# Down projection of a two-layer decoder trunk by seven half-size products instead of eight

## The chip, the cores and the metric

The kernel runs on one core of a Trainium2 chip. The metric is the device time of one launch in microseconds (us). Before the change it is 1261.44 us, the median of three runs from 1261.15 to 1261.61. A core has a matrix engine (TensorE; PE in the profile, its weight loads PEld), a vector engine (VectorE, DVE), a scalar engine (ScalarE, ACT), GpSimd (POOL), and SyncE (SP), which issues nearly all transfers here. TensorE writes its sums to PSUM, of which this kernel uses eight banks of 128 x 512 f32; everything else is in SBUF, and transfers (DMA) bring data from DRAM and back.

## The reference

Two layers (DEPTH = 2) on 512 tokens of width 1024, all f32. Each layer is attention (twelve heads of two kinds), a projection, and a SwiGLU feed-forward part between two RMS norms. The change is in the last of these:

```python
h = rms_norm(x, ffn_pre_g[l])
y = (jax.nn.silu(h @ w_gate[l]) * (h @ w_up[l])) @ w_down[l]
x = x + rms_norm(y, ffn_post_g[l])
```

w_gate and w_up are 1024 x 2816, w_down is 2816 x 1024. The last product, of a 512 x 2816 hidden matrix with w_down, is the down projection.

## The kernel before

Every product is done in three matmuls on rounded numbers: each f32 operand is split into a high part (a cast, type f32r) and a low part (operand minus high part), and high x high, high x low and low x high are summed in PSUM. A matmul takes 128 x 128 of one operand as weights and streams 128 x 512 of the other.

The weights come from DRAM in chunks of 512 KB (128 partitions x 1024 elements) through `load_w` (L245): SP issues the load into one of two landing buffers (`wr`, NRAW = 2), ScalarE casts it to `wh` (L257), VectorE subtracts to get `wl` (L258). `wh` and `wl` have three buffers each. A landing buffer is free for the next load when the subtraction is done; a `wh`/`wl` pair when TensorE's last matmul with it is done.

Feed-forward part of layer l: `gate(f)` and `up(f)` (L1195, L1198) compute the f-th 128 hidden columns for all 512 tokens, transposed (hidden columns on partitions), 24 matmuls each; `swiglu` (L1201) puts silu(gate) x up into one of eight work tiles (`half_tile`, tag w2) and splits it into `hh`, `hl`, which stay in SBUF: 22 of each. Then the down projection (L1241 to L1297). Output half 0 (512 columns) of the four token tiles t goes to four PSUM banks d0, half 1 to four banks d1. For each chunk of two f, `down_mm` does 24 matmuls (4 token tiles x 2 f x 3), 22 x 4 x 2 x 3 = 528 in a layer. When d0 is done ScalarE squares and sums it (`first_half`) while d1 runs; the last two chunks of d1 are done token tile by token tile, and the post-norm of each tile (`post_norm`, L304) runs beside the next tile's matmuls. In layer 0 the pre-norm and the transposes for layer 1's attention (`pre_norm`, `pre_T`) and its first product (`va`, with weights `wva`) follow in the same stretch.

In the attention part the order of instructions is fixed by a planner. In the feed-forward part, from the third f to the end of the down projection's loop, a scheduler of the compiler orders each engine's instructions (`pinned[0] = False`, L1229); each engine then runs its own list from top to bottom and waits on semaphores for the others.

## Time and profile before

| | |
|---|---|
| median of 3 runs | 1261.44 us |
| profiled execution | 1262.44 us, span 1260.6 us |
| TensorE busy | 1227.2 us, 97% of the span |
| VectorE, ScalarE, GpSimd busy | 52%, 42%, 17% |
| down projection, layer 0 | from 513.5 to some 632.5 us of the span |
| down projection, layer 1 | from 1131 to some 1255 us |
| loads of w_down | 44 chunks of 512 KB, 3.5 us from issue to landing (median) |
| transfers | 125.9 MB, 100 GB/s over the span |

A row of the trace gives start, duration, engine, line and what is written from what; `[3.73 <-PE d L204]` behind it says that the engine had been idle for 3.73 us and what ended that. TensorE's matmuls overlap in the pipeline, so a matmul that is shown with 389 ns takes less when others follow; the time from one start to the next is what counts.

### The profile page before, as it was taken

To read this page: it belongs to the slowest core of one execution; us is meant where nothing else is said; L and a number is where in the kernel's file an instruction comes from. 1 tells how busy PE (TensorE), PEld (TensorE's weight loads), DVE (VectorE), ACT (ScalarE), POOL (GpSimd) and SP (SyncE) were. 2 spreads that over 40 slices of the span, in tenths; PEclk is the share of its full clock that TensorE was granted. 3 is DMA by queue.
4 is the path that set the end of the run, shared out by engine and by line. 5 is a ranking of instruction groups with operands and counts; after the bars stand their busy time and mean duration, and the time that the engine had idled before them with its cause. 6 is when DMAs were issued, how large, how long until landed. Compare 5 with 4: busy or idle time off the path is not lost.

```text
span 1260.6 us, 15936 instructions
## 1 busy us (share of the span) xinstructions
PE 1227.2 (97%) x5949; PEld 1014.4 (80%) x5949; DVE 651.1 (52%) x1252; ACT 534.0 (42%) x1040; POOL 213.6 (17%) x254
## 2 busy tenths in 40 slices
PE   8999999999999999999999999999999999999998
PEld 5787877788888888888877878777988888888886
DVE  7697858673333333222458977685633333332224
ACT  5476667453222222212344757674522222222221
POOL 1302457320000000000243124672100000000001
PEclk9999999999999999999999999999999999999999
DMA  7333443403333334222513333433133333332222
GB/s 236 83 85 93 109 117 101 134 18 101 100 100 94 92 100 134 100 90 94 151 35 92 93 86 100 126 113 96 49 102 100 90 95 101 101 117 87 97 100 84
DMA packets 158717, 125.94 MB, mean 100 GB/s; under 512 B 7008, under 2 KB 134112, under 8 KB 158640
## 3 DMA queue, kind: packets, MB, share of 16 engines
q1 hardware_dynamic: 158496, 124.40, 33.0%
q8 instruction: 47, 0.77, 0.3%
q10 hardware_dynamic: 144, 0.52, 0.1%
q14 instruction: 30, 0.25, 0.1%
HBM read 114.32 MB, written 2.20 MB: 92 GB/s over the span
## 4 chain that ended last, share of the span: by engine, by line
PE 50%; issue 31%; DVE 13%; ACT 4%; POOL 1%; DMA 0%; DVEq 0%; POOLq 0%; SPq 0%; ACTq 0%
PE pj_g L204 10%; PE pj_u L204 10%; PE d L204 9%; PE o L204 4%; PE va L204 3%; PE pj_kf L204 2%; PE pj_kd L204 2%; PE pj_qf L204 1%; PE vb L204 1%; DVE t2kd L735 1%; PE ptf L209 1%; PE sf L204 1%; DVE ed L954 1%; PE of L204 1%; DVE ae L1033 1%
## 5 line engine op out<-in xcount | busy, mean ns | idle before, releaser
L204 PE MATMUL pj_g<-hT_h,wh_g 128*128 128x512 f32 (+1 forms) x384 | 142.9, 372 | 0.0
L204 PE MATMUL pj_g<-hT_h,wl_g 128*128 128x512 f32 (+1 forms) x384 | 142.6, 371 | 0.0
L204 PE MATMUL pj_g<-hT_l,wh_g 128*128 128x512 f32 (+1 forms) x384 | 142.6, 371 | 0.0
L204 PE MATMUL pj_u<-hT_h,wh_u 128*128 128x512 f32 (+1 forms) x368 | 140.1, 381 | 0.0
L204 PE MATMUL pj_u<-hT_l,wh_u 128*128 128x512 f32 (+1 forms) x368 | 139.8, 380 | 0.0
L204 PE MATMUL pj_u<-hT_h,wl_u 128*128 128x512 f32 (+1 forms) x368 | 139.7, 380 | 0.0
L258 DVE TENSOR_TENSOR wl_u<-wr_u,wh_u 128x1024 fp32r<-128x1024 f32 x44 | 53.9, 1225 | 149.8 <-ACT wh_u L257 149.8
L204 PE MATMUL d<-wh_d,hh 128*128 128x512 f32 x336 | 130.8, 389 | 0.0
L204 PE MATMUL d<-wh_d,hl 128*128 128x512 f32 x336 | 130.7, 389 | 0.0
L204 PE MATMUL d<-wl_d,hh 128*128 128x512 f32 x336 | 130.7, 389 | 0.0
L258 DVE TENSOR_TENSOR wl_d<-wr_d,wh_d 128x1024 fp32r<-128x1024 f32 x42 | 51.4, 1225 | 147.4 <-ACT wh_d L257 146.8
L257 ACT CAST wh_u<-wr_u 128x1024 fp32r<-128x1024 f32 x44 | 46.3, 1053 | 157.6 <-PE pj_g L204 147.8
L257 ACT CAST wh_d<-wr_d 128x1024 fp32r<-128x1024 f32 x42 | 44.2, 1054 | 157.6 <-PE d L204 134.3
L257 ACT CAST wh_g<-wr_g 128x1024 fp32r<-128x1024 f32 x44 | 46.3, 1053 | 146.2 <-issue 124.7
L1206 DVE TENSOR_TENSOR sg<-pj_u,sg 128x512 f32<-128x512 f32 x44 | 30.4, 692 | 141.4 <-PE pj_u L204 141.4
L204 PEld LDWEIGHTS pj_g<-hT_h,wl_g 128*128 128x128 f32 x384 | 72.4, 189 | 12.5
L204 PEld LDWEIGHTS pj_g<-hT_l,wh_g 128*128 128x128 f32 x384 | 72.3, 188 | 12.5
L204 PEld LDWEIGHTS pj_g<-hT_h,wh_g 128*128 128x128 f32 x384 | 72.3, 188 | 12.5
L204 PEld LDWEIGHTS pj_u<-hT_h,wh_u 128*128 128x128 f32 x368 | 69.3, 188 | 13.1
L204 PEld LDWEIGHTS pj_u<-hT_h,wl_u 128*128 128x128 f32 x368 | 69.1, 188 | 13.1
L204 PEld LDWEIGHTS pj_u<-hT_l,wh_u 128*128 128x128 f32 x368 | 69.2, 188 | 12.9
L204 PEld LDWEIGHTS d<-wh_d,hl 128*128 128x128 f32 x336 | 63.1, 188 | 13.2
(273 smaller groups left out, 2686.0 us busy)
## 6 DMA issues: line engine op xcount, KB each, us to landing
wr_g<-in_w_gate_dram SPq DMA_DIRECT2D x44, 512.0 KB, 3.8
wr_u<-in_w_up_dram SPq DMA_DIRECT2D x44, 512.0 KB, 3.8
wr_d<-in_w_down_dram SPq DMA_DIRECT2D x44, 512.0 KB, 3.5
wr_o<-in_w_out_dram SPq DMA_DIRECT2D x16, 512.0 KB, 4.3
wr_kd<-in_w_in_dram SPq DMA_DIRECT2D x8, 512.0 KB, 4.0
wr_qd<-in_w_in_dram SPq DMA_DIRECT2D x8, 512.0 KB, 4.2
...
wr_kf<-in_w_in_dram SPq DMA_DIRECT2D x8, 512.0 KB, 4.0
```

Source lines behind the costliest of these rows:

```text
L204: ins = PE.matmul(out, a, b, start=start, stop=stop)
L209: ins = PE.transpose(out, a, idn)
L257: A.copy(hi, raw)
L258: (eng or V).tensor_sub(lo, raw, hi.bitcast(F32))
L735: return V.tensor_mul(b["t2"], b["t2"], sinT)
L954: return V.scalar_tensor_tensor(e0, e0, b["r"][:, 0:1], e1, op0=ALU.mult, op1=ALU.add)
L1033: return V.tensor_scalar_mul(b["e"][:, :n], b["e"][:, :n], b["l"])
L1206: V.tensor_mul(sg, pu, sg)
```

## The change

The hidden matrix A (512 tokens x 2816) and w_down B (2816 x 1024) are each cut in four quarters, A11 (tokens 0 to 255, hidden columns 0 to 1407), A12, A21, A22 and B11, ..., and the output in four quarters of 256 tokens x 512 columns. One level of Strassen's scheme with 15 sums makes the four out of seven products of quarter size: with S1 = A21 + A22, S2 = S1 - A11, S3 = A11 - A21, S4 = A12 - S2 and T1 = B12 - B11, T2 = B22 - T1, T3 = B22 - B12, T4 = T2 - B21 (here with its sign turned), these are A11 B11, A12 B21, S2 T2, S1 T1, S3 T3, S4 B22 and A22 T4, and seven more sums put them together.

- *Gate/up:* f goes 0, 11, 1, 12, ... (`ORDER`), so that the four parts of a hidden block of 128 are there after each pair. `swiglu` then makes S1 to S4. A11, A12, S1 and S2 are split (`put`) into SBUF operands `op0`, `op1`, `op3`, `op2`; S3, S4 and A22 go to DRAM (`s_d`). `weight_sums` reads four 128 x 512 blocks of w_down, makes the four weight sums on VectorE and writes them to DRAM (`t_d`).
- *Down:* `product(banks, g, x)` multiplies operand `op{g}` (256 tokens) with weight side x (0 to 3 are `t_d`, 4 to 7 are quarters of w_down) over 11 blocks of 128 in six chunks, the last of half size; it fills two banks. A chunk of two blocks has 12 matmuls, a product 66. `reload` fetches S3, S4, A22 from DRAM and splits them into `op0`, `op1`, `op2` when these are free. Between products VectorE or ScalarE copies or sums the banks into `u`, `c11`, `u3`, `p5`. The norms of token tiles 0 and 1 come ahead of the seventh product, those of 2 and 3 at its end.

```diff
-TAIL = 4
+FH, TH = FT // 2, S // 2
+ORDER = [f + FT // 2 * z for f in range(FT // 2) for z in range(2)]
...
+TAIL = 3
...
-WSTAGS = ("hl12", "hl13", "hl14", "hl15")
...
+            t_d = dpool.tile([4, FH * P, S], F32, name=f"t_d{l}", tag="t_d")
+            s_d = dpool.tile([3, FH, P, TH], F32, name=f"s_d{l}", tag="s_d")
+            wd, opd = wd_d[l], {}
...
+            def put(g, f, src):
+                if f % 2 == 0:
+                    opd[g, f // 2] = operand(g, f // 2)
+                x = opd[g, f // 2][:, f % 2]
+                A.copy(x[:, 0], src)
+                V.tensor_sub(x[:, 1], src, x[:, 0].bitcast(F32))
+            def weight_sums(f):
+                b11, b12, b21, b22 = (half_tile(f"b{l}{f}{x}") for x in range(4))
+                for x, t in enumerate((b11, b12, b21, b22)):
+                    r = (f + FH * (x // 2)) * P
+                    nc.sync.dma_start(t, wd[r:r + P, CH[x % 2]])
+                V.tensor_sub(b11, b12, b11)
+                V.tensor_sub(b12, b22, b12)
+                V.tensor_sub(b22, b22, b11)
+                V.tensor_sub(b21, b21, b22)
+                for x, t in enumerate((b11, b22, b12, b21)):
+                    nc.sync.dma_start(t_d[x, f * P:(f + 1) * P], t)
...
+                if f < FH:
+                    first[f] = sg
+                    put(0, f, sg[:, :TH])
+                    return
+                f -= FH
+                a11, a21, a12, a22 = (x[:, c] for x in (first.pop(f), sg) for c in (slice(0, TH), slice(TH, S)))
+                put(1, f, a12)
+                nc.sync.dma_start(s_d[2, f], a22)
+                w = half_tile(f"s12{l}{f}")
+                s1, s2 = w[:, :TH], w[:, TH:]
+                V.tensor_add(s1, a21, a22)
+                V.tensor_sub(s2, s1, a11)
+                put(3, f, s1)
+                put(2, f, s2)
+                w = half_tile(f"s34{l}{f}")
+                s3, s4 = w[:, :TH], w[:, TH:]
+                V.tensor_sub(s3, a11, a21)
+                V.tensor_sub(s4, a12, s2)
+                nc.sync.dma_start(s_d[0:2, f].rearrange("x p n -> p x n"), w.rearrange("p (x n) -> p x n", x=2))
+                weight_sums(f)
...
-            for f in range(2, FT):
+            for f in ORDER[2:]:
...
-            def down_mm(bank, w, f, t):
-                tk = slice(t * P, (t + 1) * P)
-                for kk in range(2):
-                    mm(bank, hid[f + kk][0][:, tk], w[0][kk], f + kk == 0, False)
-                    mm(bank, hid[f + kk][0][:, tk], w[1][kk], False, False)
-                    mm(bank, hid[f + kk][1][:, tk], w[0][kk], False, f + kk == FT - 1)
...
-            d0 = [bank_t(f"d0{l}0"), bank_t(f"d0{l}1"), bank_s(f"d0{l}2"), bank_s(f"d0{l}3")]
-            d1 = [bank_g(f"d1{l}{t}") for t in range(NT)]
-            for f in range(0, FT, 2):
-                w = down_w(0, f)
-                for t in range(NT):
-                    down_mm(d0[t], w, f, t)
-            s2s = [first_half(t, d0[t], f"fp{l}") for t in range(NT)]
-            for f in range(0, FT - TAIL, 2):
-                w = down_w(1, f)
-                for t in range(NT):
-                    down_mm(d1[t], w, f, t)
...
+            def chunk_w(x, q, dst=None):
+                n = min(2, FH - 2 * q)
+                src = side(x)[2 * q * P:(2 * q + n) * P].rearrange("(k p) n -> p k n", p=P)
+                return load_w(src, [P, n, S], f"d{l}{x}{q}", dst=dst)
+            def product_mm(bank, g, q, w, m):
+                a = opd[g, q]
+                tk = slice(m * P, (m + 1) * P)
+                n = a.shape[1]
+                for k in range(n):
+                    s, e = q == k == 0, q == QN - 1 and k == n - 1
+                    mm(bank, a[:, k, 0, tk], w[0][:, k], s, False)
+                    mm(bank, a[:, k, 0, tk], w[1][:, k], False, False)
+                    mm(bank, a[:, k, 1, tk], w[0][:, k], False, e)
+            def product(banks, g, x, qs=None):
+                for q in qs or range(QN):
+                    w = chunk_w(x, q)
+                    for m in range(2):
+                        product_mm(banks[m], g, q, w, m)
+            def reload(g, s):
+                for q in range(QN):
+                    n = min(2, FH - 2 * q)
+                    raw = half_tile(f"rs{l}{s}{q}")[:, :n * TH].rearrange("p (k n) -> p k n", k=n)
+                    nc.sync.dma_start(raw, s_d[s, 2 * q:2 * q + n].rearrange("k p n -> p k n"))
+                    x = opd[g, q] = operand(g, q)
+                    A.copy(x[:, :, 0], raw)
+                    V.tensor_sub(x[:, :, 1], raw, x[:, :, 0].bitcast(F32))
+            QN = (FH + 1) // 2
+            A_, C_, B_ = ([mk(f"d{x}{l}{m}") for m in range(2)] for x, mk in (("a", bank_t), ("c", bank_s),
+                                                                             ("b", bank_g)))
+            name = f"fp{l}"
+            s2s, ys = {}, {}
+            product(A_, 0, 4)
+            u = [half_tile(f"u{l}{m}") for m in range(2)]
+            for m in range(2):
+                A.copy(u[m], A_[m])
+            product(C_, 1, 6)
+            reload(0, 0)
+            c11 = [half_tile(f"c11{l}{m}") for m in range(2)]
+            for m in range(2):
+                V.tensor_add(c11[m], C_[m], u[m])
+                s2s[m] = first_half(m, c11[m], name)
+            product(A_, 2, 1)
+            for m in range(2):
+                V.tensor_add(u[m], A_[m], u[m])
+            reload(1, 1)
+            product(B_, 3, 0)
+            p5, y, u3, y2 = (hp.tile([P, 2, S], F32, name=f"{x}{l}", tag=f"op3{q}") for q, x in enumerate(
+                ("p5", "y0", "u3", "y2")))
+            for m in range(2):
+                A.copy(p5[:, m], B_[m])
+            reload(2, 2)
+            for t in range(2):
+                ys[t] = y[:, t]
+                V.tensor_mul(ys[t], c11[t], g_fpost[:, CH[0]])
+            product(A_, 0, 2)
+            for m in range(2):
+                V.tensor_add(u3[:, m], A_[m], u[m])
+                V.tensor_add(u[m], p5[:, m], u[m])
+            product(B_, 1, 7)
+            last = l + 1 == DEPTH
+            for m in range(2):
+                V.tensor_add(u[m], B_[m], u[m])
+            for t in range(2):
+                post_norm(t, u[t], s2s[t], g_fpost, name, y=ys[t], store=last)
+                if not last:
+                    hs[t] = pre_norm(t, g_apre, f"a{l + 1}")
+            for m in range(2):
+                ys[2 + m] = y2[:, m]
+                V.tensor_add(ys[2 + m], u3[:, m], p5[:, m])
+                s2s[2 + m] = first_half(2 + m, ys[2 + m], name, z=1)
+                V.tensor_mul(ys[2 + m], ys[2 + m], g_fpost[:, CH[1]])
+            product(A_, 2, 3, range(QN - TAIL))
+            ws = [chunk_w(3, q) for q in range(QN - TAIL, QN)]
...
+            for m in range(2):
+                t = 2 + m
+                for w, q in zip(ws, range(QN - TAIL, QN)):
+                    product_mm(A_[m], 2, q, w, m)
+                    if m and not last and q == QN - TAIL:
+                        pre_T(0, hs[0], a)
+                c21 = half_tile(f"c21{l}{m}")
+                V.tensor_add(c21, A_[m], u3[:, m])
+                post_norm(t, c21, s2s[t], g_fpost, name, z=0, y=ys[t], store=last)
+                if not last:
+                    hs[t] = pre_norm(t, g_apre, a)
...
```

The compiled order shows where the sums stand. First VectorE, before, at the change from half 0 to half 1 of layer 0 (`wl_d0` and two more figures is layer 0's chunk: half, then f; the last figures are buffer numbers):

```order
L258 TENSOR_TENSOR wl_d0018_4949<-wr_d0018_4947,wh_d0018_4948 128x1024
L258 TENSOR_TENSOR wl_d0020_4979<-wr_d0020_4977,wh_d0020_4978 128x1024
L258 TENSOR_TENSOR wl_d010_5021<-wr_d010_5019,wh_d010_5020 128x1024
L258 TENSOR_TENSOR wl_d012_5051<-wr_d012_5049,wh_d012_5050 128x1024
L258 TENSOR_TENSOR wl_d014_5081<-wr_d014_5079,wh_d014_5080 128x1024
L258 TENSOR_TENSOR wl_d016_5111<-wr_d016_5109,wh_d016_5110 128x1024
```

Then VectorE now, from the third product to the fourth (`wl_d01` and a figure are chunks of the third product, `wl_d00` of the fourth; `op` and `rs` belong to a reload; `da` are the two banks of the third product):

```order
L259 TENSOR_TENSOR wl_d015_5305<-wr_d015_5303,wh_d015_5304 128x512
L1327 TENSOR_TENSOR op21070_5462<-rs021_5460,op21070_5462 128x2x256
L1327 TENSOR_TENSOR op22071_5467<-rs022_5465,op22071_5467 128x2x256
L1327 TENSOR_TENSOR op23072_5472<-rs023_5470,op23072_5472 128x2x256
L1327 TENSOR_TENSOR op24073_5477<-rs024_5475,op24073_5477 128x2x256
L1346 TENSOR_TENSOR u00_5067<-da00_4959,u00_5067 128x512
L1346 TENSOR_TENSOR u01_5068<-da01_4960,u01_5068 128x512
L259 TENSOR_TENSOR wl_d000_5349<-wr_d000_5347,wh_d000_5348 128x1024
L259 TENSOR_TENSOR wl_d001_5367<-wr_d001_5365,wh_d001_5366 128x1024
```

Before, subtractions follow each other with nothing between; now the two sums of the finished banks stand ahead of the next product's first subtraction, here as after products 2, 5 and 6.

ScalarE, before, at the same change of halves (`junk` are the squares of the four finished banks):

```order
L257 CAST wh_d0020_4978<-wr_d0020_4977 128x1024
L257 CAST wh_d010_5020<-wr_d010_5019 128x1024
L257 CAST wh_d012_5050<-wr_d012_5049 128x1024
L276 ACTIVATE junk31_5008,s2_fp00_5007<-d000_4669 128x512
L276 ACTIVATE junk32_5011,s2_fp01_5010<-d001_4670 128x512
L276 ACTIVATE junk33_5014,s2_fp02_5013<-d002_4671 128x512
L276 ACTIVATE junk34_5017,s2_fp03_5016<-d003_4672 128x512
L257 CAST wh_d014_5080<-wr_d014_5079 128x1024
```

ScalarE now, from the first product (`wh_d04`) to the second (`wh_d06`):

```order
L258 CAST wh_d044_5038<-wr_d044_5037 128x1024
L258 CAST wh_d045_5056<-wr_d045_5055 128x512
L1337 COPY u00_5067<-da00_4959 128x512
L1337 COPY u01_5068<-da01_4960 128x512
L258 CAST wh_d060_5072<-wr_d060_5071 128x1024
L258 CAST wh_d061_5090<-wr_d061_5089 128x1024
L1326 CAST op00055_5175<-rs000_5173 128x2x256
L1326 CAST op01056_5180<-rs001_5178 128x2x256
L1326 CAST op02057_5185<-rs002_5183 128x2x256
L1326 CAST op03058_5190<-rs003_5188 128x2x256
L258 CAST wh_d062_5108<-wr_d062_5107 128x1024
```

The squares stood behind two casts of the new half; the two copies of the finished banks `da` stand ahead of the second product's first cast, and four casts of a reload ahead of its third.

VectorE in layer 1, before, where half 1 ends (`y0` are products of d0 with the gain, `whl` the low parts of the chunk that is kept apart):

```order
L258 TENSOR_TENSOR wl_d1114_10462<-wr_d1114_10460,wh_d1114_10461 128x1024
L258 TENSOR_TENSOR wl_d1116_10492<-wr_d1116_10490,wh_d1116_10491 128x1024
L1276 TENSOR_TENSOR y010_10536<-d010_9900,g_fpost1_9898 128x512
L1276 TENSOR_TENSOR y011_10537<-d011_9901,g_fpost1_9898 128x512
L258 TENSOR_TENSOR wl_d1120_10532<-wr_d1120_10530,wh_d1120_10531 128x1024
L1276 TENSOR_TENSOR y012_10538<-d012_9902,g_fpost1_9898 128x512
L263 TENSOR_TENSOR whl14118_10524<-wr_d1118_10520,whl12118_10522 128x512
L263 TENSOR_TENSOR whl15118_10525<-wr_d1118_10520,whl13118_10523 128x512
L1276 TENSOR_TENSOR y013_10539<-d013_9903,g_fpost1_9898 128x512
```

VectorE now, from layer 1's sixth product (`wl_d17`) to the seventh (`wl_d13`):

```order
L259 TENSOR_TENSOR wl_d175_11344<-wr_d175_11342,wh_d175_11343 128x512
L1364 TENSOR_TENSOR u10_10726<-db10_10622,u10_10726 128x512
L1364 TENSOR_TENSOR u11_10727<-db11_10623,u11_10727 128x512
L313 TENSOR_TENSOR y1_fp10_11358<-u10_10726,g_fpost1_10616 128x512
L313 TENSOR_TENSOR y1_fp11_11370<-u11_10727,g_fpost1_10616 128x512
L316 SCALAR_TENSOR_TENSOR xs_78<-y01_11109,r_fp10_11360,xs_78 128x512
L316 SCALAR_TENSOR_TENSOR xs_78<-y1_fp10_11358,r_fp10_11360,xs_78 128x512
L316 SCALAR_TENSOR_TENSOR xs_78<-y01_11109,r_fp11_11372,xs_78 128x512
L316 SCALAR_TENSOR_TENSOR xs_78<-y1_fp11_11370,r_fp11_11372,xs_78 128x512
L1373 TENSOR_TENSOR y21_11111<-y21_11111,g_fpost1_10616 128x512 x2
L259 TENSOR_TENSOR wl_d130_11392<-wr_d130_11390,wh_d130_11391 128x1024
```

Two sums, two products with the gain, four updates of `xs` and two more products with the gain now stand between the last subtraction of the sixth product and the first of the seventh.

## Rows read from the trace of the kernel before

**Rows 1.** Part 1 of the page: busy us, share of the span, instructions.
```profile
PE 1227.2 (97%) x5949; PEld 1014.4 (80%) x5949; DVE 651.1 (52%) x1252; ACT 534.0 (42%) x1040; POOL 213.6 (17%) x254
```

**Rows 2.** Chain of waits, 500 to 670 us: start, us, what, how many.
```profile
513.86 111.53 PE d L204 x492
```

**Rows 3.** Stages: us; busy PE, PEld, DVE, ACT, POOL (instructions); PEclk, DMA share, GB/s.
```profile
265.00:510.00 245.00, 245.00 (x1162) 206.18 (x1161) 92.92 (x106) 77.09 (x108) 4.29 (x9) 1.00 0.33 97
513.50:632.50 119.00, 118.43 (x525) 97.88 (x524) 37.62 (x37) 32.36 (x47) 8.99 (x10) 1.00 0.33 106
1131.00:1255.00 124.00, 123.39 (x545) 101.87 (x543) 35.19 (x37) 26.94 (x38) 2.58 (x6) 1.00 0.26 89
```

**Rows 4.** Tile wr_d: min/median/max ns of readers, us to landing.
```profile
L257 ACT CAST wh_d<-wr_d x42: 1042/1055/1058, 502.8 to 1233.2; 128x1024 fp32r<-128x1024 f32 x42
L258 DVE TENSOR_TENSOR wl_d<-wr_d,wh_d x42: 1214/1225/1226, 503.9 to 1234.3; 128x1024 fp32r<-128x1024 f32 x42
...
DMA to landing us min/median/max: 3.3/3.5/4.9
```

**Rows 5.** Timeline of VectorE and of SP about 581 us.
```profile
580.26 1.23 DVE L258 TENSOR_TENSOR wl_d<-wr_d,wh_d 128x1024 fp32r<-128x1024 f32 x1 [3.56 <-ACT wh_d L257]
...
581.51 0.37 SPq L256 DMA_DIRECT2D wr_d<-in_w_down_dram  x1
```

**Rows 6.** Timeline of ScalarE at the change of halves, layer 0.
```profile
568.29 1.05 ACT L257 CAST wh_d<-wr_d 128x1024 fp32r<-128x1024 f32 x1 [4.38 <-PE d L204]
...
573.82 0.60 ACT L276 ACTIVATE junk<-d 128x512 f32<-128x512 f32 x1 [0.67 <-PE d L204]
...
574.40 1.04 ACT L257 CAST wh_d<-wr_d 128x1024 fp32r<-128x1024 f32 x1
```

**Rows 7.** Groups by line: what one instruction lasts (mean ns).
```profile
L276 ACT ACTIVATE junk<-d 128x512 f32<-128x512 f32 x16 | 9.6, 598 | 33.4 <-PE d L204 33.3
...
L312 DVE SCALAR_TENSOR_TENSOR xs<-y,r_fp,xs 128x512 f32<-128x512 f32 x8 | 6.0, 746 | 1.8 <-POOL r_fp L271 1.8
...
L791 DVE TENSOR_TENSOR vf<-vb,vf 128x256 fp32r<-128x256 f32 x16 | 5.7, 417 | 4.3 <-ACT vf L787 4.3
...
L1276 DVE TENSOR_TENSOR y<-d,g_fpost 128x512 f32<-128x512 f32 x8 | 5.5, 686 | 3.9 <-PE d L204 3.9
...
L990 ACT COPY mixd<-od 128x512 f32<-128x512 f32 x8 | 4.7, 583 | 0.0
```

**Rows 8.** DMA issues at 598 to 613 us, and of a gain row.
```profile
DMA packets 1962, 3.68 MB, mean 245 GB/s; under 512 B 174, under 2 KB 174, under 8 KB 1961
...
wr_d<-in_w_down_dram SPq DMA_DIRECT2D x3, 512.0 KB, 4.9
...
g_apre<-in_attn_pre_g_dram SPq DMA_DIRECT2D x1, 512.0 KB, 6.0
```

**Rows 9.** Timeline after the last matmul.
```profile
1254.00 0.39 PE L204 MATMUL d<-wh_d,hl 128*128 128x512 f32 x1
1254.49 0.60 ACT L276 ACTIVATE junk<-d 128x512 f32<-128x512 f32 x1 [2.03 <-PE d L204]
...
1255.27 0.30 POOL L270 TENSOR_SCALAR v_fp<-s_fp 128x1 f32<-128x1 f32 x1 [1.77 <-ACT junk L276]
1255.65 0.56 POOL L271 TENSOR_TENSOR r_fp<-v_fp,nhalf 128x1 f32<-128x1 f32 x1
```

**Rows 10.** TensorE's gap at 231 us, and the granted clock (PEclk) after it.
```profile
230.66 0.40 PE L204 MATMUL o<-wh_o,hT_l 128*128 128x512 f32 x1
233.14 0.30 PE L209 MATMUL ptf<-con,ae 128*128 128x128 f32 x1 [2.08 <-DVE ae L1033]
...
234.00:235.00 1.00, 1.00 (x4) 0.82 (x3) 1.00 (x5) 1.00 (x3) 0.00 (x0) 0.58 0.71 183
235.00:236.00 1.00, 1.00 (x4) 0.60 (x3) 0.96 (x3) 0.83 (x3) 0.00 (x0) 0.50 1.05 304
237.00:238.00 1.00, 1.00 (x5) 0.79 (x4) 0.85 (x3) 0.93 (x1) 0.00 (x0) 0.71 0.02 5
```

114 lines of the change are left out of this document (46 added, 68 removed).

## The prediction

> **What bounds the kernel now.** I read the page first, then the chain of waits through the feed-forward part of layer 0, then the table by stage, and only then single instructions. The page shows TensorE busy for 97% of the span [rows 1]; the chain through the down projection is one piece, 492 matmuls in 111.53 us with nothing between them [rows 2]. So a 512-column matmul costs 111.53/492 = 0.2267 us there, and the stage is bound by their number: 22 x 4 x 2 x 3 = 528 of them, 119.7 us in each layer. VectorE and ScalarE are a third busy in it and the DMA engines a third [rows 3]. None of the three is near a limit, so the question is how much slack the *chain* through them has. A chunk's way: a weight chunk of 128 x 1024 lands, ScalarE casts it (wh), VectorE subtracts (wl), and when the subtraction is done SP issues the next load into that buffer: cast 1.055, subtraction 1.225, subtraction end 581.49 to next issue 581.51 [rows 4, 5]. There are two landing buffers (wr) and three of wh and wl. With a landing of 3.5 us [rows 4] and some 0.1 us of hand-overs, one buffer's round is R = 3.5 + 1.055 + 1.225 + 0.1 = 5.9 us, so a chunk can come every 2.95 us. Before, a chunk feeds 24 matmuls, 5.44 us: the chain sleeps half the time, and nothing that is queued in it hurts. The rows at the change of halves show it: ScalarE's four squares of the finished banks wait for TensorE, the next cast stands behind them and starts at 574.40, 6.1 us after its forerunner, and the matmuls go on unbroken [rows 6].
>
> **The change part by part.**
>
> Removed: seven products of 11 x 2 x 3 = 66 matmuls are 462 instead of 528. 66 x 0.2267 = 14.96 us a layer, **-29.9 us** for both. The Trainium skill, "TensorE: Matmul & The Clock Gate", section Back-to-back issue gap, puts a sustained 512-column matmul at about 131 ns; by that, 132 matmuls would bring only 17.3 us. The trace has 0.2267, and the measurement decides.
>
> Gate/up: for a pair of f (four chunks, 21.8 us of TensorE) VectorE does 4 subtractions of 1.225, two products and two splits of 0.69, 7.7 us, as its 38% in the stage says [rows 3]. Added: 4 sums of weights of 0.69, and four 256-column splits and four sums instead of the two splits, about 0.42 each by the 256-column row [rows 7]: +4.8 us, 57%. The loads get 2.5 MB a pair on top of 2.1, some 210 GB/s, where the trace has stretches of 245 and over [rows 8]. SP now waits between loads for sums; a chunk here lasts 5.44 us and the buffers hold two to three chunks, over 10 us, and the waits in the order of SP are under 9 by the same rows. I take 0, hidden by TensorE; up to +1 us a pair (22 in all) if that cover is too thin, no gain.
>
> The down stage: a chunk now feeds 2 token tiles, 12 matmuls, 2.72 us, against the 2.95 of the chain. Two costs follow.
>
> (a) *Boundaries.* The order puts each product's bank sums on VectorE (or copies on ScalarE) ahead of the next product's first subtraction, as the pieces of the order show. Both engines take instructions in order [rows 6], so that product cannot start its low half before the last matmul of the one before has been read. From the rows: a reader starts 0.26 us after the last matmul's slot (issued 1254.00, slot end 1254.23, ACT 1254.49) [rows 9]; a bank sum or product 0.69, a copy 0.58, a scaled sum (xs) 0.75 [rows 7]; the first bank of a product is ready three matmuls, 0.68, earlier; from one engine to the next 0.1, an estimate between the 0.02 and the 0.26 of [rows 5, 9]; two matmuls of the next chunk need wh alone and run ahead, -0.45.
> 1 to 2: 0.26 + copy 0.58 + cast 1.055 + subtraction 1.225 + 0.2 - 0.45 = 2.85.
> 2 to 3 and 3 to 4: 0.26 + 0.69 + 1.225 + 0.1 - 0.45 = 1.8 each.
> 4 to 5 (the copy of the first bank alone stands ahead): 2.15.
> 5 to 6 (u3 and u, three sums after the last bank): 0.26 + 3 x 0.69 + 1.225 + 0.1 - 0.45 = 3.2.
> 6 to 7, layer 0: sum, y product, subtraction: 0.26 + 2 x 0.69 + 1.225 + 0.1 - 0.45 = 2.5. Inside product 7 the subtractions of its third and fifth chunk stand behind the norms of tokens 0 and 1 (two xs and two h of the same form, with ScalarE's square and POOL's 0.30 + 0.56 [rows 7, 9] waited for between): by laying these end to end the third is ready 11.9 us after product 6 and needed at 8.4, the fifth is 1.5 late: 4.5 together, less the early matmuls of the third.
> 6 to 7, layer 1: ahead of wl stand the second sum, two y products, four xs, two y2 products: 0.26 + 0.69 + 1.38 + 3.0 (and 0.2 of waiting) + 1.38 + 1.225 + 0.1 - 0.45 = 7.8.
> Layer 0: 2.85 + 1.8 + 1.8 + 2.15 + 3.2 + 2.5 + 4.5 = 18.8; layer 1: 2.85 + 1.8 + 1.8 + 2.15 + 3.2 + 7.8 = 19.6. **+38.4 us.** All of these durations but the 0.1 are in the trace; with the two waits inside layer 0's product 7 gone it would be 34.
>
> (b) *The round.* Chunks 3 and 5 of a product need a buffer that chunks 1 and 3 free, so from the first wl a product lasts 2R + 10 matmuls + a half chunk = 2R + 3.63, against 14.96 - 0.45 = 14.51. At R = 5.9: 15.43, +0.9. The landing is what I cannot read: the new stage moves 20.2 MB of weights and 4.3 MB of reloaded sums in some 125 us, 196 GB/s (layer 0 another 3 MB), and a product with a reload nearer 245. In the stretch at 245 GB/s wr_d landed in 4.9 [rows 8], in the calm ones in 3.5, at best 3.3 [rows 4]. So +0.5 to +3.7 a product; I take 3.8 us, nearer the calm rows because TensorE's own waits thin the loads: +1.5 for ten products (2 to 6, both layers), **+15 us**; ends +5 and +37. The Trainium skill, "DMA: Bandwidth & Descriptors", section Latency and other measured facts, has HBM access grow from 0.2 us to 2 at high load; by it the landing would be 5.3, an estimate, and this term +45. The trace agrees in kind, with 4.9.
>
> The first product: its weights are there, but VectorE's last sums of weights (four of 0.69, after reads of the last pair) stand before wl of chunk 5, which by the rows comes at the moment it is needed, 10.9 us in. In layer 0 the two gain rows (512 KB each, 6 us [rows 8]) are issued ahead of product 2's first load: +1.5 over the 2.85. **+1.5**, ends 0 and 4.
>
> (c) *The clock.* TensorE idled 2.08 us up to 233.14, and its granted clock then fell to 0.50 (1.2 of 2.4 GHz) and was back four microseconds on, which cost some 1.7 us [rows 10]. Some three gaps of a layer are as long. Where the round is late anyway half of it is covered: 0.8 x 6 = 5, or 0 if the early matmuls split the gaps: **+2.5**.
>
> The end: after the last matmul one more sum (c21, 0.69) stands before the squares of the last tile [rows 9]: **+0.7**. The hand-over from layer 0 to 1 has norms of tokens 0 and 1 done earlier; and 66 matmuls of va, 15 us, before the last token's transposes are asked for, against some 8.5 us of norms: I take 0.
>
> Sum: -29.9 + 38.4 + 15 + 1.5 + 2.5 + 0.7 = **+28 us**. Against the profiled execution of before, 1262.4 us (span 1260.6 and 1.8 around it), that is 1290.6; it lies 1.0 above the median of the runs, 1261.4, so some 1289.5 there. The five terms are partly covers of one another (a late chunk uses up a half-speed stretch), so I take **1288**.
>
> **Rivals.**
> 1. *Fewer matmuls win.* The three wh/wl pairs and two wr buffers run ahead of TensorE far enough for each product to start on ready chunks; the point that decides is (29.9 - 0.7)/12 = 2.4 us a boundary, round included; with nothing but the matmuls it would be 1261.4 - 29.2 = 1232, with half the boundary price and a landing of 3.3, 1261.4 - 29.2 + 19 + 5 = 1256. For it: in the trace TensorE never waits for wl_d. Against: that has 5.44 us a chunk, and the order of the sums is fixed. 0.12, of it 0.04 within 0.2%.
> 2. *The loads bind.* Landing 4.9 throughout: 1261.4 + 28 + 22 = 1311; at 4.5, 1303. For it the stretch in [rows 8]; against, TensorE's waits thin the demand. 0.15.
> 3. *The clock falls at each of the 12 boundaries*, 1.7 us uncovered: 1289.5 + 18 = 1307. For it [rows 10]; against, most gaps are under 2.08 and split. 0.08.
> 4. *Gate/up gets late* behind the sums, 1 us a pair: 1310. 0.05.
> Forecast: 0.60, its own range 1274 to 1299.
>
> **How the numbers follow.** A measurement of this kernel can tell 0.2%, 2.5 us. Slower: 0.60 + 0.15 + 0.08 + 0.05 = 0.88; same 0.04; faster 0.08. The low end of the range is boundaries at 34, landing at 3.3 and no clock loss, 1261.4 - 29.2 + 34 + 5 = 1271, taken 2 lower, 1269; the high end lets in most of rivals 2 and 3, 1308.
>
> **What would show it.** Right: TensorE busy with 5,820 or so matmuls but idle some 55 us in the two down stages; waits of TensorE for VectorE's wl_d at the top of the list, with pieces of 2 to 3 us at the product boundaries and 7 to 8 us before layer 1's seventh; the chain there running through VectorE and the loads; wr_d landing between 3.5 and 4.5; gate/up still 5.44 us a chunk. Wrong: products of 14.9 us on end, TensorE without gaps (rival 1), landings of 5 (2), a granted clock well under 0.97 in the down stages (3), gaps in gate/up (4).

## The result and the profile after

The changed kernel takes 1303.8 us, the median of four runs from 1299.0 to 1308.6, against 1261.5 of the kernel before in the same comparison: 1.0336 times as long, 95% interval 1.0293 to 1.0378. That is +42.3 us where +26.5 was forecast, 16 more. The direction held, and the time lies in the range from 1269 to 1308, but not in the part of it that the forecast gave as its own, 1274 to 1299: it lies where rival 2 was (1303). The profiled execution took 1306.31 us (span 1304.5) against 1262.44.

The first part of the page of the changed kernel (busy time, share, instructions), and the table by stage, which answers to [rows 1, 3] (columns as there; the last three are granted clock, DMA share, GB/s):

```profile
PE 1227.0 (94%) x5817; PEld 998.2 (77%) x5817; DVE 818.3 (63%) x1574; ACT 600.7 (46%) x1162; POOL 209.9 (16%) x250
```

```profile
265.00:510.00 245.00, 245.00 (x1161) 206.09 (x1160) 132.14 (x202) 78.93 (x122) 3.02 (x6) 1.00 0.62 194
510.00:660.00 150.00, 128.83 (x509) 98.04 (x508) 90.31 (x114) 68.68 (x105) 9.37 (x14) 0.93 0.62 196
1154.00:1300.00 146.00, 119.66 (x465) 90.18 (x463) 79.01 (x99) 56.72 (x81) 4.32 (x8) 0.93 0.57 186
```

The 132 matmuls are gone (5949 to 5817), and yet TensorE is busy as long as before, 1227.0 us against 1227.2: 132 matmuls fewer at 0.2267 would have left 1197.3 us, so those that are left are shown with some 30 us more than before. Its idle time went from 33 to 78 us (span less busy time). Gate/up shows no gap, with twice the traffic (194 GB/s). All of the loss is in the two down stages, where the clock falls to a mean of 0.93: from the first to the last matmul they take 141.1 and 142.0 us, where it was 121.2 and 119.5.

TensorE's waits in these stages, from the timelines of its engine (start, duration, what, and in brackets the idle time before and what ended it), and the clock around some of them (551 to 557 stands behind the wait of 1.46):

```profile
523.27 0.50 PE L205 MATMUL da<-wl_d,op 128*128 128x512 f32 x1 [0.76 <-DVE wl_d L259]
531.17 1.22 PE L205 MATMUL dc<-wh_d,op 128*128 128x512 f32 x2 [3.76 <-ACT wh_d L258]
551.28 0.50 PE L205 MATMUL da<-wl_d,op 128*128 128x512 f32 x1 [1.46 <-DVE wl_d L259]
570.88 0.61 PE L205 MATMUL db<-wl_d,op 128*128 128x512 f32 x1 [0.97 <-DVE wl_d L259]
609.35 0.79 PE L205 MATMUL db<-wl_d,op 128*128 128x512 f32 x1 [1.98 <-DVE wl_d L259]
639.79 0.80 PE L205 MATMUL da<-wl_d,op 128*128 128x512 f32 x1 [3.14 <-DVE wl_d L259]
...
1278.85 0.79 PE L205 MATMUL da<-wl_d,op 128*128 128x512 f32 x1 [6.88 <-DVE wl_d L259]
```

```profile
531.00:537.00 6.00, 5.79 (x13) 4.10 (x14) 4.86 (x6) 4.39 (x7) 0.00 (x0) 0.50 0.91 272
537.00:540.00 3.00, 3.00 (x15) 2.46 (x14) 1.27 (x2) 1.22 (x3) 0.00 (x0) 1.00 0.66 216
551.00:557.00 6.00, 5.72 (x25) 4.49 (x25) 4.48 (x6) 3.93 (x7) 0.00 (x0) 1.00 0.72 252
570.00:576.00 6.00, 5.12 (x15) 4.05 (x16) 2.89 (x4) 1.83 (x3) 0.00 (x0) 0.72 0.53 167
609.00:615.00 6.00, 5.65 (x13) 4.46 (x14) 3.75 (x5) 2.09 (x2) 0.00 (x0) 0.50 0.43 162
639.00:645.00 6.00, 5.21 (x17) 4.18 (x17) 5.05 (x7) 4.07 (x10) 1.42 (x2) 0.72 0.43 131
1279.00:1284.00 5.00, 5.00 (x12) 3.94 (x13) 1.19 (x2) 1.08 (x2) 0.00 (x0) 0.50 0.64 210
```

The waits are where the forecast put them: at the boundaries, 6.88 us of them ahead of the first `wl` of layer 1's seventh product, and in layer 0's seventh before its third chunk (3.14). At eleven of the twelve changes of product TensorE waits first for the cast of the next chunk, and at eight of these ScalarE had waited with that cast for the transfer. Behind five of the waits the clock is at half, 1.2 GHz, for up to six microseconds.

Two rounds of the landing buffers in the fourth product, which answer to [rows 4, 5] (ScalarE, VectorE, and the DMA queue of SyncE, SPq):

```profile
570.85 0.36 SPq L257 DMA_DIRECT2D wr_d<-t_d  x1
571.98 0.36 SPq L257 DMA_DIRECT2D wr_d<-t_d  x1
574.32 1.05 ACT L258 CAST wh_d<-wr_d 128x1024 fp32r<-128x1024 f32 x1 [3.54 <-DMA wr_d<-t_d]
575.40 1.23 DVE L259 TENSOR_TENSOR wl_d<-wr_d,wh_d 128x1024 fp32r<-128x1024 f32 x1 [3.11 <-ACT wh_d L258]
576.66 0.36 SPq L257 DMA_DIRECT2D wr_d<-t_d  x1
576.85 1.05 ACT L258 CAST wh_d<-wr_d 128x1024 fp32r<-128x1024 f32 x1 [1.48 <-DMA wr_d<-t_d]
577.82 0.69 DVE L1356 TENSOR_TENSOR y<-c,g_fpost 128x512 f32<-128x512 f32 x1 [1.19 <-PE db L205]
578.43 1.22 DVE L259 TENSOR_TENSOR wl_d<-wr_d,wh_d 128x1024 fp32r<-128x1024 f32 x1
579.67 0.33 SPq L257 DMA_DIRECT2D wr_d<-t_d  x1
```

The first buffer's round is 576.66 - 570.85 = 5.81, the second's 579.67 - 571.98 = 7.69: its landing is longer (cast at 576.85, 4.9 after the issue), and its subtraction stands behind the product `y`, which VectorE took first. Issued loads and landings in the page (KB each, median us):

```profile
wr_d<-t_d SPq DMA_DIRECT2D x40, 512.0 KB, 3.8
wr_d<-in_w_down_dram SPq DMA_DIRECT2D x30, 512.0 KB, 4.5
rs<-s_d SPq DMA_DIRECT2D x30, 256.0 KB, 5.4
```

### The profile page after: what moved, and what is told of

Same layout as the page of the kernel before. It is cut to its first block, busy times and chain, and to the rows that moved or that the text cites. A ratio compares the mean times of both kernels' runs of the same rounds, so it can differ in the third digit from the quotient of the medians.

```text
span 1304.5 us, 16741 instructions
## 1 busy us (share of the span) xinstructions
PE 1227.0 (94%) x5817; PEld 998.2 (77%) x5817; DVE 818.3 (63%) x1574; ACT 600.7 (46%) x1162; POOL 209.9 (16%) x250
## 4 chain that ended last, share of the span: by engine, by line
PE 42%; issue 34%; DVE 15%; ACT 5%; DMA 3%; POOL 2%; POOLq 0%; DVEq 0%; ACTq 0%; SPq 0%
PE pj_g L205 9%; PE pj_u L205 9%; PE o L205 4%; PE va L205 3%; PE pj_kf L205 2%; DMA wr_d<-in_w_down_dram 2%; PE pj_kd L205 2%; PE db L205 1%; PE dc L205 1%; PE pj_qf L205 1%; PE vb L205 1%; DVE ed L958 1%; DVE ed L875 1%; DVE t2kd L739 1%; PE of L205 1%
## 5 line engine op out<-in xcount | busy, mean ns | idle before, releaser
L259 DVE TENSOR_TENSOR wl_d<-wr_d,wh_d 128x1024 fp32r<-128x1024 f32 x84 | 94.3, 1134 | 97.5 <-ACT wh_d L258 96.8
L258 ACT CAST wh_d<-wr_d 128x1024 fp32r<-128x1024 f32 x84 | 81.9, 977 | 148.4 <-DMA wr_d<-t_d 70.1
L271 POOL TENSOR_SCALAR v_fp<-s_fp 128x1 f32<-128x1 f32 x8 | 4.5, 559 | 741.1 <-ACT junk L277 387.2
L205 PE MATMUL da<-wh_d,op 128*128 128x512 f32 x352 | 116.1, 405 | 6.7 <-ACT wh_d L258 6.7
L205 PE MATMUL da<-wl_d,op 128*128 128x512 f32 x176 | 73.8, 419 | 19.9 <-DVE wl_d L259 19.6
L205 PEld LDWEIGHTS da<-wh_d,op 128*128 128x128 f32 x352 | 68.3, 195 | 24.5 <-ACT wh_d L258 10.9
```

The source lines that it names most:

```text
L205: ins = PE.matmul(out, a, b, start=start, stop=stop)
L258: A.copy(hi, raw)
L259: (eng or V).tensor_sub(lo, raw, hi.bitcast(F32))
L271: G.tensor_scalar(v, s2[:, 0:1], scalar1=s2[:, 1:2], scalar2=EPS, op0=ALU.add, op1=ALU.add)
```

## The experiments

Every kernel was timed beside the kernel before. That one's median differs between the comparisons (1256.9 to 1262.1), so the last column, the difference to it, is what is compared here.

| kernel | median | ratio, 95% interval | to before |
|---|---|---|---|
| changed kernel | 1303.8 | 1.0336 (1.0293 to 1.0378) | +42.3 |
| unread matmuls in the waits | 1304.7 | 1.0352 (1.0331 to 1.0373) | +42.6 |
| sums behind two subtractions | 1306.3 | 1.0356 (1.0330 to 1.0382) | +44.2 |
| half chunks | 1281.8 | 1.0155 (1.0128 to 1.0181) | +19.7 |
| no reloads | 1296.7 | 1.0286 (1.0259 to 1.0314) | +34.6 |
| weight sums and gains early | 1295.5 | 1.0309 (1.0278 to 1.0340) | +37.3 |
| six work tiles | 1297.9 | 1.0311 (1.0282 to 1.0339) | +40.0 |
| six tiles, three landing buffers | 1252.2 | 0.9953 (0.9936 to 0.9970) | -5.9 |
| the same with half chunks | 1258.5 | 0.9998 (0.9985 to 1.0011) | +0.4 |
| the same, sums first | 1280.5 | 1.0172 (1.0136 to 1.0208) | +23.5 |
| the same, sums first, unread matmuls | 1275.9 | 1.0143 (1.0110 to 1.0176) | +19.0 |
| kernel before, six tiles, three buffers | 1259.4 | 1.0012 (0.9998 to 1.0026) | +1.5 |
| three buffers, early, seventh product reordered | 1241.2 | 0.9860 (0.9839 to 0.9881) | -16.6 |

**Is it the clock?** Unread matmuls fill the waits between products.

```diff
+            spare = bank_g(f"fill{l}")
+            def fill(n):
+                pinned[0] = True
+                for _ in range(n):
+                    mm(spare, hT_h[:, 0, :P], hT_h[:, 1], True, True)
+                pinned[0] = False
             product(A_, 0, 4)
+            fill(8)
```

> The changed kernel, and between the products (where TensorE waits) 14, 6, 8, 6, 8 and 8 matmuls of 512 columns that nobody reads, on a spare bank; 30 of them ahead of layer 1's seventh product. They fill the waits that the changed kernel has there (3.8, 1.5, 1.7, 1.5, 2.4, 1.8 and 6.9 us) with work, at 0.227 each, and take no wait away. Theory A, the clock is what was sized wrong: TensorE's granted clock no longer falls behind these waits (in layer 0 the falls from 531 to 537, at 571 and at 609 go, the one at 640 inside the seventh product stays), the span's mean goes from 0.977 to 0.988 or more, and the time from 1304 to 1288-1294. Rival B, the half-speed stretches are covered, since the weights come too late anyway: the clock rises as much, TensorE idles more inside the products, and the time stays within 4 us of 1304.

The kernel that ran has 8 at each boundary and 30 before layer 1's last product (the expectation names 14, 6, 8, 6, 8 and 8). The first row below is TensorE's work in the first down stage with them, the other two are rows at the change from the fifth to the sixth product:

```profile
510.00:660.00 150.00, 136.79 (x569) 105.15 (x568) 91.64 (x116) 69.12 (x105) 11.11 (x16) 0.98 0.61 197
```

```profile
605.90 1.98 PE L205 MATMUL fill<-hT_h 128*128 128x512 f32 x8
609.18 0.50 PE L205 MATMUL db<-wl_d,op 128*128 128x512 f32 x1 [0.85 <-DVE wl_d L259]
```

The clock came back, from 0.93 to 0.98 in the stage and from 0.977 to 0.991 over the span, and the time did not move (+42.6 against +42.3). The sixth product's first wl arrives at 609.18, where it was 609.35 without. Rival B: a matmul at half speed costs nothing when the weights for the next ones are not there yet. The unread matmuls themselves did not make TensorE late to hide a gain: at eight of the twelve changes a wait is left behind them, and at the other four they take 1.81 us where the wait, counted from start to start, was 1.6 to 2.0.

**Is it the order at the boundaries?** Each product's sums are put behind the subtractions of the next product's first two chunks (an order edge on the sums). The edit also moves each reload in the program from behind a product into it.

```diff
             def product(banks, g, x, qs=None):
                 for q in qs or range(QN):
                     w = chunk_w(x, q)
                     for m in range(2):
                         product_mm(banks[m], g, q, w, m)
+                    if q == 1:
+                        while late:
+                            late.pop(0)()
...
-            for m in range(2):
-                V.tensor_add(u[m], A_[m], u[m])
-            reload(1, 1)
+            def sum_3():
+                for m in range(2):
+                    pin(V.tensor_add(u[m], A_[m], u[m]))
+                reload(2, 2)
+            late.append(sum_3)
```

> The changed kernel with the bank sums and copies of each product put behind the subtractions of the next product's first two chunks. Theory A, the boundaries cost what the forecast says, as sums that stand ahead of the first subtraction: 0.58 at 1 to 2, 0.7 at 2 to 3 and 3 to 4, 2.1 at 5 to 6, 1.4 and 6.0 at 6 to 7 (layer 0, layer 1): some 14 us of waits for both layers, and with the clock that falls behind them up to 25: 1280-1290. Rival B, VectorE and the two landing buffers are the bound, and sums that are moved only make a later chunk late: the waits move into the products, 1298-1308.

No gain, rival B's range. In the trace the first subtraction now stands ahead of the sums at all twelve changes, and the waits there (added up from the brackets) fall from 31.5 to 17.1 us. What is left, at ten of the changes, is above all a wait for the cast, and at six of these the cast waits for its load, as from the third to the fourth product:

```profile
571.21 1.04 ACT L258 CAST wh_d<-wr_d 128x1024 fp32r<-128x1024 f32 x1 [1.64 <-DMA wr_d<-t_d]
572.29 1.22 DVE L259 TENSOR_TENSOR wl_d<-wr_d,wh_d 128x1024 fp32r<-128x1024 f32 x1 [1.99 <-ACT wh_d L258]
572.31 0.74 PE L205 MATMUL db<-wh_d,op 128*128 128x512 f32 x2 [1.27 <-ACT wh_d L258]
```

The rest has moved into the products, above all the seventh (26.1 us from its third matmul to the end of its last in layer 0, where it was 22.0, and 21.2 in layer 1, where it was 17.8). The pace of the loads gives a likely reason: a product takes six loads, three rounds of each of two buffers, and in the changed kernel a round lasted 6.25 us on average from product 2 to 5 of layer 0 (23 steps from 532.40 to 604.25), which is 18.75 a product. That it would be as much wherever the sums stand is argued, not shown.

**Is it the round?** Halves, no reloads, and a third buffer.

```diff
-                return load_w(src, [P, n, S], f"d{l}{x}{q}", dst=dst)
...
+                for k in range(n):
+                    nc.sync.dma_start(w[0][:, k], src[:, k])
+                for k in range(n):
+                    A.copy(w[1][:, k], w[0][:, k])
+                    V.tensor_sub(w[2][:, k], w[0][:, k], w[1][:, k].bitcast(F32))
+                return w[1:]
```

> The changed kernel, each 128 x 1024 chunk of the down projection loaded, cast and subtracted as two halves of 128 x 512 (two transfers into the same landing buffer). The first half is ready a cast and a subtraction of 512 after its landing (0.58 + 0.69 in place of 1.06 + 1.23), the second half's cast runs beside the first half's subtraction: the round of a buffer goes from 3.8 + 2.4 to some 3.8 + 1.9. Theory A, the round and the first chunk's chain bind: some 1.0 us less at each of 12 boundaries and 0.5-1 a product in the round, with the clock 1270-1285. Rival B, the transfers themselves bind (294 to 370 GB/s in parts of the stage): the landings take as long or longer with twice as many transfers, and the time stays at 1300-1310.

22.6 us less, theory A's range: the landings are 3.2 and 3.8 for a half (3.8 and 4.5 for the whole), and the second half's cast runs beside the first half's subtraction. But the order changed too, which the edit does not say: in both layers, at the changes 2 to 3, 4 to 5, 5 to 6 and 6 to 7, the next product's first subtraction or cast now stands ahead of the sums or copies, as here on VectorE from layer 1's fifth product to its sixth (L1308 is the subtraction, L1367 a sum; the sixth starts at 1226.38):

```profile
1225.14 1.29 DVE L1308 TENSOR_TENSOR wl_d<-wr_d,wh_d 128x512 fp32r<-128x512 f32 x2 [0.34 <-ACT wh_d L1307]
1226.35 0.68 DVE L1367 TENSOR_TENSOR u<-da,u 128x512 f32<-128x512 f32 x1
```

So the shorter round and the order share the 22.6 us, in parts that no run tells.

```diff
-            reload(0, 0)
...
-            reload(1, 1)
...
-            reload(2, 2)
```

> The changed kernel without the reloads of S3, S4 and A22: products 5, 6 and 7 use the operands that op0, op1 and op2 still hold, so 18 transfers of 256 KB, 18 casts and 18 subtractions a layer are left out (the sums are other numbers). Theory A, the reloads crowd the loads, ScalarE and VectorE in products 2 to 4: their lengths (18.0 to 21 us) fall to some 17, 6-8 us a layer, and 1288-1292 in all. Rival B, the reloads hide in the waits: each of these products within 0.5 us of what it was, 1300-1306.

7.7 us less, between the two theories (A had 6 to 8 a layer), with overlapping intervals of the ratios: in layer 0 the third product, from its first matmul to the next one's, goes from 20.0 to 18.8 us and the sixth from 21.6 to 19.7, and layer 1's third from 21.1 to 18.0. The rest of the round is there without the reloads.

```diff
-NRAW, NW2, NRC = 2, 8, 2
+NRAW, NW2, NRC = 3, 6, 2
```

> The changed kernel with three landing buffers in place of two; for their room there are six work tiles (w2) in place of eight, in the whole kernel. In the changed kernel a new weight load goes out every 3.12 us from product 2 to 5 of layer 0 (532.40 to 604.25, 23 steps), a round of 6.25 us for two buffers. Theory A, this round is the pace: with three buffers it would allow 2.1 us a chunk, under the 2.72 of TensorE, products 2 to 6 go from 18-21 to 16.8-17.5 us, 20 us less in all: 1280-1287 (what fewer work tiles cost elsewhere is read in the other stages). Rival B, VectorE and ScalarE, which take sums, reloads and chunks in order, are the pace whatever has landed: the products as long, 1300-1306.

48.2 us less, more than twice what theory A allowed, and 0.5% under the kernel before, with the interval of the ratio clear of 1. The stages and the landings of this kernel, and VectorE at the change from the third to the fourth product:

```profile
510.00:628.00 118.00, 111.06 (x472) 88.16 (x471) 84.41 (x105) 63.82 (x94) 6.93 (x10) 0.97 0.78 250
1129.00:1250.00 121.00, 108.70 (x464) 87.35 (x462) 79.31 (x100) 56.33 (x81) 4.73 (x8) 0.97 0.68 224
```

```profile
wr_d<-t_d SPq DMA_DIRECT2D x40, 512.0 KB, 4.5
wr_d<-in_w_down_dram SPq DMA_DIRECT2D x30, 512.0 KB, 4.3
```

```profile
557.75 1.23 DVE L259 TENSOR_TENSOR wl_d<-wr_d,wh_d 128x1024 fp32r<-128x1024 f32 x1 [0.27 <-ACT wh_d L258]
558.89 0.68 DVE L1346 TENSOR_TENSOR u<-da,u 128x512 f32<-128x512 f32 x1
559.49 1.22 DVE L259 TENSOR_TENSOR wl_d<-wr_d,wh_d 128x1024 fp32r<-128x1024 f32 x1
560.62 0.68 DVE L1346 TENSOR_TENSOR u<-da,u 128x512 f32<-128x512 f32 x1
```

The landings are about as long (4.5 and 4.3, where it was 3.8 and 4.5) at 250 GB/s, and TensorE waits some 2 us a layer in the first six products. And here again the order changed: with a third buffer the compiler's scheduler puts the next product's first subtraction (557.75) ahead of the sum (558.89); with two it stood behind. Why it does is not shown; that it counts on the chunk being ready early is my guess. So two causes sit in one number.

The control for the tiles, and the kernel before with the same line:

> The changed kernel with two landing buffers, as it was, and six work tiles in place of eight: the other half of the edit that gave 1252.2 us with three landing buffers. Theory A, the third landing buffer alone brought the 51 us: 1300-1310 here. Rival B, the number of work tiles sets when reloads and sums are issued and brought part of it: under 1295.

> The kernel before the change with three landing buffers and six work tiles. Theory A, a chunk of 24 matmuls never waits there, so a third buffer brings nothing in the down projection: 1256-1263, and the comparison of 1252.2 with the kernel before is fair. Rival B, the third buffer helps the attention part or gate/up as well: under 1254, and Strassen's scheme then has to be held against that.

Six tiles alone, between the ranges of the two theories, bring 2.3 us with overlapping intervals, which can't be told from nothing; the kernel before gains nothing (+1.5). The third buffer matters to the changed kernel alone.

**The two causes apart.** Three buffers, with the order of the sums put back.

```diff
+            lead = []
             def product(banks, g, x, qs=None):
                 for q in qs or range(QN):
-                    w = chunk_w(x, q)
+                    with tc.issue_after(lead.pop()) if lead else nullcontext():
+                        w = chunk_w(x, q)
...
-                V.tensor_add(u[m], A_[m], u[m])
+                lead[:] = [V.tensor_add(u[m], A_[m], u[m]).ins]
```

> Three landing buffers and six work tiles (1252.2 us), with the order at the boundaries that the forecast priced: each product's bank sums or copies stand ahead of the next product's first subtraction or cast, as they do with two buffers; with three the compiler's scheduler had put the first subtractions ahead of the sums. Nothing else is changed. Theory A, the order at the boundaries is a cost of its own, as the forecast has it: waits of 2.9, 1.8, 1.8, 2.9, 3.2 and 2.0 us, 14.5 a layer against 1.5 a layer that three buffers have there now: 1252 + 26 = 1278, TensorE idle in these places and its clock falling behind some of them (1278-1290). Rival B, with weights landed in time the chain catches up and the boundaries cost under a half of that: 1252-1265.

TensorE's waits at layer 1's boundaries 3 to 4 and 4 to 5 of this kernel:

```profile
1194.73 0.50 PE L205 MATMUL db<-wl_d,op 128*128 128x512 f32 x1 [3.03 <-DVE wl_d L259]
1212.75 0.73 PE L205 MATMUL da<-wh_d,op 128*128 128x512 f32 x2 [1.62 <-ACT wh_d L258]
1214.01 0.50 PE L205 MATMUL da<-wl_d,op 128*128 128x512 f32 x1 [0.53 <-DVE wl_d L259]
```

+29.4 us, where the forecast's boundary terms give 26. The waits are 2.15, 1.47, 3.03, 2.15, 2.67 and 2.67 us in layer 1, against 2.9, 1.8, 1.8, 2.9, 3.2 and 2.0. One is off: at 3 to 4 ScalarE's cast of a reload, which waited for its transfer, stood ahead of the chunk's cast. So the order is a cost of its own once the round has slack, and 40.0 - 23.5 = 16.5 us (six tiles with two buffers against this kernel) is what the third buffer brings with the sums in front. Not all of the order is the same: in layer 1's seventh product the norms now stand behind the first subtraction, with waits of 2.67 and 3.38 in place of one of 7.01 with two buffers and six tiles, and at 4 to 5 both copies stand ahead of the cast, where it was one.

> The same kernel, sums first, with 10, 6, 6, 10, 12 and 7 unread matmuls of 512 columns at the six boundaries of each layer: under the waits that the forecast gives (2.3, 1.4, 1.4, 2.3, 2.7, 1.6 us at 0.227 each), so that they keep TensorE at work without making it later. With three buffers no late load stands behind a half-speed stretch, so this prices the clock by itself. Theory A, the clock costs some 1.5 us at each boundary of two microseconds or more: 8-18 us less than the kernel with sums first. Rival B, it costs nothing here either: within 3 us of it.

4.5 us less, between the two theories, and the intervals of the ratios overlap. The clock is worth a few tenths of a microsecond at a boundary here, if anything; more cannot be said.

**The first product.** The weight sums of a pair are made with its first f, and the gain rows fetched in gate/up.

```diff
                 if f < FH:
                     first[f] = sg
                     put(0, f, sg[:, :TH])
+                    if f:
+                        weight_sums(f)
                     return
...
-                weight_sums(f)
+                if f == 0:
+                    weight_sums(f)
...
                 swiglu(f, pg, pu)
-            g_fpost = gain(fpost_d, l, f"g_fpost{l}")
...
+                if f == 4:
+                    g_fpost = gain(fpost_d, l, f"g_fpost{l}")
...
```

> The changed kernel with two things moved: each weight sum is made one f earlier (with the first f of its pair instead of the second, so the last is made 5.4 us before the end of gate/up's last product and more) and the two gain rows are fetched in gate/up (at its tenth f) and not at the head of the down projection. Theory A, the first product (20.5 us in layer 0, 21.6 in layer 1, then 18 for the second) is late by these: both first products 17.5-18.5, 5-7 us less, 1297-1299. Rival B, a later product gives it back since the weight stream paces: within 3 us of 1304.

From its first matmul to the next product's the first product goes from 20.5 to 16.7 us in layer 0 and from 21.6 to 17.9 in layer 1. In the changed kernel's DMA queue its late loads stand like this (the write of weight sums, the gain rows, then product 2's first loads):

```profile
515.30 0.38 SPq L257 DMA_DIRECT2D wr_d<-in_w_down_dram  x1
517.42 1.71 SPq L257 DMA_DIRECT2D wr_d<-in_w_down_dram  x1
520.08 1.29 SPq L1226 DMA_DIRECT2D t_d<-b  x3
520.91 1.05 ACT L258 CAST wh_d<-wr_d 128x1024 fp32r<-128x1024 f32 x1 [6.22 <-DMA wr_d<-in_w_down_dram]
521.41 0.74 SPq L236 DMA_DIRECT2D g_fpost<-in_ffn_post_g_dram  x1
522.21 0.75 SPq L236 DMA_DIRECT2D g_apre<-in_attn_pre_g_dram  x1
523.24 1.42 SPq L257 DMA_DIRECT2D wr_d<-in_w_down_dram  x2
```

The load issued at 515.30 is cast at 520.91, 5.6 us later, and ScalarE had waited for it. Over the whole kernel 5.0 us are left of the 7.5, and the intervals overlap: part may be given back in later products.

**Together.**

> Half chunks (1281.8 us with two landing buffers) and three landing buffers with six work tiles together. Theory A, both act on the same round, which then is no longer the pace; what is left are the boundaries, the first and the seventh product: 1268-1276. Rival B, the halves gained by the shorter chain at each boundary, not by the round, and the third buffer brings its own 20 us on top: 1258-1264. Rival C, the halves have taken away all that the round cost: 1280-1284.

The number is rival B's, its reason is not: three buffers without halves are at -5.9, so the halves lose 6.3 us there. With the round out of the way, twice the transfers, casts and subtractions bring nothing; which of them costs the 6.3, or whether another order of the instructions does, was not tried.

The last kernel has three buffers without halves, the earlier weight sums and gain rows, and this order in the seventh product:

```diff
+            def norm(t):
+                tc.keep_in_program_order(V.tensor_add(u[t], B_[t], u[t]))
+                post_norm(t, u[t], s2s[t], g_fpost, name, y=ys[t], store=last)
...
             product(A_, 2, 3, range(QN - TAIL))
-            ws = [chunk_w(3, q) for q in range(QN - TAIL, QN)]
+            norm(0)
+            ws = [chunk_w(3, QN - TAIL)]
+            norm(1)
+            ws += [chunk_w(3, q) for q in range(QN - TAIL + 1, QN)]
```

> Three landing buffers and six work tiles, weight sums and gain rows earlier, and in the seventh product the norms of tokens 0 and 1 behind the subtractions of its third and fourth chunk. With three buffers TensorE still waited 0.8 + 0.5 + 0.5 us at the first change of products of layer 0, 0.2 + 0.3 + 0.8 at layer 1's, and 3.1 + 1.7 and 3.1 inside the seventh products. Theory A, these go: 1252 less 8 in the seventh products and 3 at the first ones, 1240-1244. Rival B, the norms moved back make the transposes and the end late by as much: 1249-1253.

1241.2 us, theory A's range, 0.9860 of the kernel before, and under both kernels with the interval clear of 1. The first three products of layer 0 start at 509.48, 524.44 and 539.40: 14.96 each, exactly 66 x 0.2267. What still waits there is the seventh product:

```profile
618.91 0.79 PE L205 MATMUL da<-wl_d,op 128*128 128x512 f32 x1 [4.19 <-DVE wl_d L259]
```

## Why the prediction was right, and where its size was off

Product by product, the length being the time from one product's third matmul to the next one's (its first two need `wh` alone and run ahead of the wait, as in the forecast), the seventh's to the end of its last; forecast by the prediction's terms (14.96, the boundary behind it, 1.5 of the round; in layer 0's seventh the 4.5 of waits and the 0.8 that eight transposes take there, 649.05 to 649.84) and measured:

| | 1 | 2 | 3 | 4 | 5 | 6 | 7 |
|---|---|---|---|---|---|---|---|
| layer 0, forecast | 19.3 | 18.3 | 18.3 | 18.6 | 19.7 | 19.0 | 19.8 |
| layer 0, measured | 21.3 | 18.8 | 19.6 | 18.6 | 19.9 | 20.7 | 22.0 |
| layer 1, forecast | 17.8 | 18.3 | 18.3 | 18.6 | 19.7 | 45.9 with 7 and the end | |
| layer 1, measured | 22.4 | 18.1 | 21.1 | 18.5 | 19.2 | 50.3 with 7 and the end | |

Some 19 us are missing in the forecast rows: 6.6 in the two first products, some 6 in products 2 to 6, 5.5 in the two seventh, 0.8 at the end.

- *Removed, -29.9:* right. Products with weights at hand take 14.96 us.
- *Gate/up, 0:* right (245.00 busy of 245 in the window).
- *(a) Boundaries, +38.4:* right in place and size: the waits at the twelve changes add up to 31.5 us (33.9 by the forecast), of it 0.84 + 6.88 = 7.7 before layer 1's seventh product (7.8), and the wait inside layer 0's seventh is 3.14 (3.0). The cause, the sums ahead of the first subtraction, is shown as a cost of its own by the sums-first kernel: 29.4 for the six changes of both layers (some 29 by the forecast's rows, less the 3 that three buffers still had), clock included. In the changed kernel it is only half of the story: with two buffers late loads stand at the same places (the first change of layer 0: copies done at 528.09, the cast at 530.07 after 1.98 us of waiting for its load), and moving the sums back brought nothing. So (a) and (b) were not two costs to be added up, as the forecast has them, but two causes at the same places; that their sum came as near as it did is in part luck. Nor was the order fixed, as the case against rival 1 had it: the scheduler chose another one with three buffers, and with halves.
- *(b) The round, +15, with the landing taken as 3.8:* right in kind, too small by some 6 us. The third buffer is worth 16.5 us with the sums in front and everything else late as well; the third products (1.3 and 2.8 us) and layer 0's sixth (1.7) are over their forecast, the others of 2 to 6 within 0.6. The landing of the weight sums was the 3.8 that was taken; that of w_down 4.5. What was sized wrong is R: it was landing + cast + subtraction, with an idle ScalarE and VectorE in between. The round of 7.69 us above has a landing 1.1 us longer than that and 0.5 behind `y`; leaving the reloads out shortens the third products to 18.9 and 18.0, and the whole by 7.7, with overlapping intervals. VectorE's and ScalarE's own queues should have stood in R.
- *The first product, +1.5:* too small, this is the largest relative miss. It is 2.0 and 4.6 us over its forecast; moving its cause earlier shortens it by 3.8 and 3.7. I had counted VectorE's last sums as coming "at the moment it is needed" and the landing there at its calm length, but the writes of the sums, the gain rows and the weight loads go through one queue at 270 to 370 GB/s (over 3 us each, 516 to 531), and a load landed in 5.6 us. Its upper end, 4, was for layer 0 alone.
- *(c) The clock, +2.5:* the trace looks as if this were the miss (30 us more of busy time than the matmuls need, and 0.93 in the down stages, which the forecast had named as a sign for rival 3), and the first experiment shows that it is not: with the clock at 0.991 the kernel is as slow. Layer 1's seventh product shows why one row misleads: it runs at half clock until 1284.5, which is most of the 3.3 us by which it is over; with unread matmuls ahead of it the clock stayed at 1.00 there, fell for 3.4 us later in the product, and waits for its chunks came instead (19.2 us from its third matmul to the end of its last, where it was 17.8). The prediction's reason, that the chain is late anyway and covers it, held more than the half that it took.
- *The end, +0.7:* 1.5 (last matmul's slot to the end of the span 7.9 against 6.4).
- *Rivals.* Rival 1 (fewer matmuls win) failed here, but its condition, landings that run ahead of TensorE, is what one more buffer provides (with the order that came with it), and then it wins. Rival 2 gave 1303 at a landing of 4.5 and hits the number; but with three buffers the landings are 4.5 and 4.3 and the time 1252, or 1280 with the sums in front, so it is not the landing by itself. Rival 3's falls of the clock are there and cost next to nothing. Rival 4 did not occur.

The Trainium skill, "DMA: Bandwidth & Descriptors", section Latency and other measured facts, gives the figures by which I had an estimate of 5.3 for the landing. The medians here are below it, 3.8 and 4.5, the longest 7.8. The Trainium skill, "Perfetto Trace Analysis", section Optimization Strategy, says that the same gap coming again and again on the engine that should be full can mean that there is no room to allocate the next tile. The runs agree: one landing buffer more, 4 KB per partition, took most of the gaps at the products away, in part through the order that came with it.

Left open: how the 22.6 us of the halves divide between round and order, how the 16.5 us of the third buffer divide between landing and queues, why layer 0's seventh product still waits 4.19 us in the best version, and whether work tiles play a part at all.
